# Two passes over 128 expert blocks: twelve blocks of activations kept on chip, and another pace for the work beside the first pass

## The chip, the cores and the metric

One core of one Trainium2 chip runs the whole program in one launch. The metric is the device time in microseconds; several runs of a kernel are compared by their median.

## The reference, cut to what matters

Two transformer blocks follow each other: one with a convolution, windowed attention and a layer of single-vector experts ("peer"), one with gated linear attention, sparse attention and feed-forward layers. The change lies in the expert layer:

```python
def peer(h, w_pq, sub_keys, u_emb, v_emb):
    q = (h @ w_pq).reshape(B, S, PEER_HEADS, 2, PEER_DHALF)
    sc = jnp.einsum("bshcd,hcnd->bshcn", q, sub_keys)
    s_top, i_top = lax.top_k(sc, PEER_TOPK)
    cand = s_top[..., 0, :, None] + s_top[..., 1, None, :]       # and its index
    best, pos = lax.top_k(cand, PEER_TOPK)
    gate = jax.nn.softmax(best, axis=-1)
    ...
    a = gelu(einsum("ced,cd->ce", u_emb[idx], hx))
    return einsum("ce,ced->cd", g * a, v_emb[idx])
```

There are 512 tokens of width 1024, 8 heads that choose 16 of 128 x 128 = 16384 experts each, and two tables, `u_emb` and `v_emb`, of 16384 rows of 1024 float32.

## The kernel before, in words

**Two ways to compute the layer.** For 352 tokens (`ND`) the kernel computes it densely: all 16384 activations, times a table of gates that is zero where an expert was not chosen. For the other 160 tokens it gathers the chosen rows: 128 tokens (`NF`) with one gather per chosen expert, 32 tokens (`NX`) packed four experts to a gather. That makes 128 + 32 = 160 gathers of rows of `u` and as many of `v`, each 128 rows of 1024.

**The dense passes.** Pass one runs over 128 blocks of 128 experts: `block` loads the block's weights of `peer_u` (SP's queue, three buffers `wr`), splits them into a high part `wh` (ACT, L195) and a low part `wl` (DVE, L196), and multiplies with the split tokens `hH`, `hL` in 24 matmuls of 128x352 (`three`, L216). ACT applies the gelu (L984) and stores the result to DRAM (`gd`, L985, ACT's queue). Pass two runs over the same blocks in the same order: it loads the activations of two blocks back (`g`), multiplies them with the table of gates (`w`, product `gw`, DVE, L1033), splits the product into `aH` and `aL`, and accumulates 24 matmuls with `peer_v` into eight PSUM tiles that stay open over all 128 blocks.

**Beside pass one.** A queue of small steps with costs, `self.queue`, holds what is left of the key search, the routing of each 128 tokens (`route`, DVE), and the build of the table (`spread_weights`): per four tokens a one-hot on DVE (L892, L900), others on ACT (L896, L897), eight small matmuls (L905), a copy on ACT (L906); every 16 tokens a store to DRAM (`wd`, L908). Each block of pass one runs `self.budget_u` units of that queue. Once the last 128 tokens are routed (`ready`), `chosen` issues gathers (POOL, L966) at `self.every(i)` rows a block, four buffers deep; a DVE instruction forms each dot (L943). In pass two the second gathers' rows are added up on DVE (L949), paced over all its blocks.

**Order of the work.** A planner lists the program's instructions by priority: `high_priority(n)` moves an instruction n places ahead in it, `issue_after` puts it behind another one on its engine. Each engine then works through its own list in order. Weights are `self.offset` = 90 places ahead, the loads of `g` and `w` `self.early` = 160, products and splits `self.soon` = 90. An engine with nothing due takes later work whose inputs are there. The loads of the table's first group of 16 blocks stand behind pass one in the program and are issued once the table is stored.

Of the kernel before, what the change touches and what calls it, by code (L numbers as in the profile page):

```python
# [22 lines left out]
S = 512  # L23
# [86 lines left out]
class Build:  # L110
    def __init__(self, ctx, tc, a, out):
        self.ctx, self.tc, self.nc, self.a, self.out = ctx, tc, tc.nc, a, out
        self.V, self.A, self.T, self.G = tc.nc.vector, tc.nc.scalar, tc.nc.tensor, tc.nc.gpsimd
        self.queue, self.rate, self.left, self.units = [], 0, 0, []
        self.waiting, self.rstd, self.behind = None, None, []
        self.lanes, self.credit, self.budget = [], 0, 0.8
        self.offset = 90
        self.early, self.soon, self.first = 160, 90, 60
        self.pad = 3.0

        self.on_act = lambda t: (0, 1) if t == 2 else (0, 1, 2)
        self.every = lambda i: 0.8 if i < 40 else 1.4 if i < 92 else 1.75
        self.wcost = 1.0
        self.rate_q = 4.5
        self.o2 = 40
        self.budget_u = 2.2
        self.ahead = 150
        self.sb = ctx.enter_context(tc.tile_pool(name="base", bufs=1))
        self.pp = ctx.enter_context(tc.tile_pool(name="psum", bufs=8, space=PSUM))
        self.dr = ctx.enter_context(tc.tile_pool(name="dram", bufs=1, space=DRAM))  # L130
# [542 lines left out]
    def peer(self, hs):  # L673
# [306 lines left out]
        next(rest)  # L980
        for i in range(NKEY):
            p = self.block(a["peer_u"][i], KD, hs, ND)
            g = self.tmp()
            A.activation(g[:, :ND], p[:, :ND], AF.Gelu)  # L984
            nc.scalar.dma_start(gd[i // 2][:, i % 2, :], g[:, :ND])  # L985
            self.run(self.budget_u)
            if len(self.queue) <= ready:
                budget += self.every(i)
            while budget >= 1.0 and sent < NF + NC:
                rest.send(self.last)  # L990
                sent += 1
                budget -= 1.0
        self.run()
        self.finish()
        inner.close()

# [15 lines left out]
        rounded = -(-ND // 64) * 64  # L1012
        wide = lambda tag, bufs, dt=F32: self.t(tag, rounded, bufs, dt, pool=pool)[:, :ND]
        for i in range(NKEY):

            with self.tc.high_priority(self.early):
                if i % 2 == 0:
                    g = self.t("g", 2 * ND, 3, pool=pool).rearrange("p (b n) -> p b n", b=2)
                    self.load(g, gd[i // 2])
                if i % NW == 0:  # L1020
                    w = ws.pop(0)
                    if i + NW < NKEY:
                        ws.append(weight_tile())
                if i % 2 == 0 and i // NW * NW + NW < NKEY:
                    with self.tc.issue_after(self.last_load):
                        part_of_weights(ws[0], i // NW + 1, i % NW // 2)
            with ExitStack() as near:
                near.enter_context(self.tc.high_priority(self.soon))
                if i < 2:
                    near.enter_context(self.tc.issue_after(end_u))  # L1030
                if i % 2 == 0:
                    gw = self.t("gw", 2 * ND, 2, pool=pool).rearrange("p (b n) -> p b n", b=2)
                    V.tensor_tensor(gw.rearrange("p b (u k) -> p b u k", k=TG), g.rearrange("p b (u k) -> p b u k", k=TG),  # L1033
                                    w[:, :, i % NW:i % NW + 2, :].rearrange("p u b k -> p b u k"), op=OP.mult)
                aH, aL = wide("aH", 3, F32R), wide("aL", 3, F32R)
                last = self.split(aH, aL, gw[:, i % 2, :])
            parts = self.weights(a["peer_v"][i], KD)
            for m in range(KD):
                self.three(acc[m][:, :ND], parts[m], (aH, aL), i == 0, i == NKEY - 1)
            while sent < min(n_sends, n_u + (n_sends - n_u) * (i + 1) / (NKEY - 3)):  # L1040
# [623 lines left out]
```

## Time and profile before

| what | us |
| --- | --- |
| median of 3 runs (3052.92 to 3059.8) | 3054.82 |
| the profiled execution | 3058.59 |
| its span | 3056.7 |
| PE busy in the span | 2973.7 (97%) |
| DVE busy | 2211.8 (72%) |
| ACT busy | 1314.8 (43%) |
| POOL busy | 478.9 (16%) |

Times in the views below count from the span's start. A busy PE is not PE at its peak: matmuls overlap, so what PE loses in a stretch is read by counting its matmuls. PEclk is the share of its clock that was granted; DMA is the mean busy share of the 16 DMA engines.

### The profile page before, as it was taken

Reading aid. Unit: us, or ns where it says so; the run is one execution under the profiler, and the core shown is the slowest. Engines: PE = TensorE matmul, PEld = TensorE weight load, DVE = VectorE, ACT = ScalarE, POOL = GpSimd, SP = SyncE. Lnnn points to the kernel's source line nnn. Section 1 sums busy time; section 2 is a strip of 40 time slices with the busy share of each in tenths; the row PEclk is TensorE's granted clock in tenths of the full one; section 3 lists DMA queues with packets and bytes.
Section 4 is the critical chain, followed back from the end, with each engine's and each line's share of the span. In section 5 each row is a group of like instructions: output and inputs, shape, how many; then the busy total and the mean of one; then the engine's idle time right before and its main releaser. Section 6 shows DMA issues by size and latency. Waiting matters only on the chain.

```text
span 3056.7 us, 41903 instructions
## 1 busy us (share of the span) xinstructions
PE 2973.7 (97%) x15549; PEld 2598.2 (85%) x15549; DVE 2211.8 (72%) x4115; ACT 1314.8 (43%) x2310; POOL 478.9 (16%) x338
## 2 busy tenths in 40 slices
PE   8999999999999998999999999999999999999998
PEld 7877788898999988999999888887788877888887
DVE  6999868999878677899989744434976655544435
ACT  5347542347888433333333422224333354323223
POOL 0000000022433454555555000000000000000000
PEclk9999999999999999999999999999999999999999
DMA  5321232387999999999999322333223334222232
GB/s 179 104 77 62 69 97 89 107 273 245 357 350 349 378 372 381 390 398 400 399 398 382 104 97 98 102 114 99 77 76 104 131 104 131 96 97 97 92 96 103
DMA packets 201716, 586.28 MB, mean 192 GB/s; under 512 B 21016, under 2 KB 64344, under 8 KB 198696
## 3 DMA queue, kind: packets, MB, share of 16 engines
q1 hardware_dynamic: 128944, 361.47, 34.1%
q0 software_dynamic: 46480, 168.14, 14.8%
q10 hardware_dynamic: 26088, 54.01, 4.9%
q8 instruction: 122, 2.00, 0.3%
q14 instruction: 82, 0.67, 0.1%
HBM read 523.94 MB, written 60.29 MB: 191 GB/s over the span
## 4 chain that ended last, share of the span: by engine, by line
PE 62%; DVE 18%; DMA 8%; issue 7%; POOL 3%; ACT 2%; DVEq 0%; POOLq 0%; ACTq 0%; SPq 0%
PE ps L216 54%; DMA wr<-in_peer_v_dram 4%; DVE wl L196 4%; POOL row L966 3%; DVE c L488 3%; PE ps L905 2%; PE ps L1287 1%; DMA g<-gd 1%; DVE topi L720 1%; DVE row L943 1%; DMA row<-in_peer_v_dram,rows 1%; PE ps L1324 1%; DVE top L719 1%; DVE tok L949 1%; ACT wh L195 1%
## 5 line engine op out<-in xcount | busy, mean ns | idle before, releaser
L195 ACT CAST wh<-wr 128x1024 fp32r<-128x1024 f32 (+1 forms) x560 | 584.3, 1044 | 1410.5 <-PE ps L216 668.2
L216 PE MATMUL ps<-hH,wh 128*128 128x512 f32 (+1 forms) x2792 | 1039.8, 373 | 8.1 <-ACT wh L195 6.1
L216 PE MATMUL ps<-hH,wl 128*128 128x512 f32 (+1 forms) x2792 | 1026.0, 368 | 20.1 <-DVE wl L196 20.0
L216 PE MATMUL ps<-hL,wh 128*128 128x512 f32 (+1 forms) x2792 | 1022.5, 366 | 1.6 <-DVE hL L196 1.4
L196 DVE TENSOR_TENSOR wl<-wr,wh 128x1024 fp32r<-128x1024 f32 (+1 forms) x560 | 678.8, 1213 | 253.4 <-ACT wh L195 251.0
L216 PEld LDWEIGHTS ps<-hH,wl 128*128 128x128 f32 x2792 | 527.0, 189 | 97.5 <-DVE wl L196 27.7
L216 PEld LDWEIGHTS ps<-hH,wh 128*128 128x128 f32 x2792 | 527.3, 189 | 83.3 <-ACT wh L195 7.8
L216 PEld LDWEIGHTS ps<-hL,wh 128*128 128x128 f32 x2792 | 527.6, 189 | 72.1 <-DVE hL L196 3.5
L216 PE MATMUL ps<-aL,wh 128*128 128x352 f32 (+1 forms) x1376 | 469.1, 341 | 5.3 <-DVE aL L196 5.3
L216 PE MATMUL ps<-aH,wh 128*128 128x352 f32 (+1 forms) x1376 | 467.6, 340 | 3.3 <-ACT aH L195 2.0
L216 PE MATMUL ps<-aH,wl 128*128 128x352 f32 (+1 forms) x1376 | 468.4, 340 | 0.6 <-DVE wl L196 0.6
L966 POOL DMA_INDIRECT row<-in_peer_rows_dram,rows x128 | 172.8, 1350 | 933.1 <-DVE topi L720 615.7
L216 PEld LDWEIGHTS ps<-aL,wh 128*128 128x128 f32 x1376 | 258.6, 188 | 23.6 <-DVE aL L196 9.5
L216 PEld LDWEIGHTS ps<-aH,wh 128*128 128x128 f32 x1376 | 259.5, 189 | 18.0 <-ACT aH L195 2.6
L216 PEld LDWEIGHTS ps<-aH,wl 128*128 128x128 f32 x1376 | 258.5, 188 | 14.5 <-DVE wl L196 0.9
L966 POOL DMA_INDIRECT row<-in_peer_v_dram,rows x128 | 202.5, 1582 | 186.9 <-DVE tok L949 159.3
L943 DVE CUSTOM_DVE_ANT_0 row<-row,tok 128x1024 f32<-128x1024 f32 x160 | 193.2, 1219 | 43.2 <-DMA row<-in_peer_rows_dram,rows 25.0
L488 DVE SCALAR_TENSOR_TENSOR c<-up,cw,c 128x512 f32<-128x512 f32 x240 | 171.4, 743 | 0.8
L949 DVE SCALAR_TENSOR_TENSOR tok<-row,dots,tok 128x1024 f32<-128x1024 f32 x127 | 162.4, 1278 | 4.3 <-DMA row<-in_peer_v_dram,rows 3.6
L216 PE MATMUL ps<-c,wh 128*128 128x512 f32 x384 | 126.4, 410 | 0.0
L1099 DVE TENSOR_TENSOR tmp<-ps,rstd 128x512 f32<-128x512 f32 x44 | 30.4, 691 | 129.8 <-PE ps L216 129.8
L905 PE MATMUL ps<-ohr,ohl 128*128 128x128 f32 x704 | 96.2, 275 | 2.6 <-DVE ohl L900 2.0
(353 smaller groups left out, 3061.0 us busy)
## 6 DMA issues: line engine op xcount, KB each, us to landing
wr<-in_peer_u_dram SPq DMA_DIRECT2D x128, 512.0 KB, 5.8
wr<-in_peer_v_dram SPq DMA_DIRECT2D x128, 512.0 KB, 8.4
wr<-in_ffn_w_in_dram SPq DMA_DIRECT2D x88, 512.0 KB, 3.2
wr<-in_mix_w_in_dram SPq DMA_DIRECT2D x46, 512.0 KB, 3.3
gd<-tmp ACTq DMA_DIRECT2D x128, 176.0 KB, 5.7
wd<-wb ACTq DMA_DIRECT2D x22, 1024.0 KB, 6.8
g<-gd SPq DMA_DIRECT2D x64, 352.0 KB, 8.2
wr<-in_w_in_dram SPq DMA_DIRECT2D x42, 512.0 KB, 3.5
```

The source lines that it names most:

```text
L195: self.A.copy(H, src)
L196: return self.V.tensor_sub(L, src, H.bitcast(F32)).ins
L216: self.T.matmul(ps, l, r, start=first and i == 0, stop=last and i == 2)
L488: V.scalar_tensor_tensor(y, u[:, w:w + S], cw[:, i:i + 1], y, op0=OP.mult, op1=OP.add)
L719: V.max(v[:, o], sl)
L720: V.max_index(ix[:, o], v[:, o], sl)
L905: T.matmul(pw[:, k * 128:k * 128 + 128], l4[:, k], r4[:, k], start=True, stop=True)
L943: V.tensor_tensor_reduce(out=g, in0=g, in1=h, scale=1.0, scalar=0.0, op0=OP.mult, op1=OP.add, accum_out=d[:, j:j + 1])
L949: V.scalar_tensor_tensor(sums[-1], g, d[:, j:j + 1], sums[-1], op0=OP.mult, op1=OP.add)
L966: G.indirect_dma_start(out=g, out_offset=None, in_=tables[i], in_offset=at)
L1287: T.matmul(pv[t], l[:, tok[t]], rr[:, s], start=k0 + k + n == 0, stop=k0 + k == KD - 1 and n == 2)
L1324: T.matmul(p[:, t * 64:t * 64 + 64], E[:, tok[t]], ql[:, t * 64:t * 64 + 64], start=True, stop=True)
```

## The change

Three things change.

- Paces. Rows per block of pass one: 1.2 up to block 40 and 1.4 after, where they were 0.8, 1.4 (from 40) and 1.75 (from 92). Units of the queue per block: 2.6 until the last tokens are routed and 1.9 after, where they were 2.2.
- The last twelve blocks of pass one write their activations to six tiles in SBUF (`kept`) instead of DRAM. For that the queue is emptied and the routing's memory closed ahead of block 116, not behind block 127.
- Pass two takes the blocks in another order: 116 to 127 from `kept`, then 112 to 115, then 0 to 111. The six tiles then serve as buffers for the activations that are loaded (three before). The split halves `aH`, `aL` take the eight buffers `hH`, `hL`, which pass one's tokens held, in place of three of their own.

```diff
-        self.every = lambda i: 0.8 if i < 40 else 1.4 if i < 92 else 1.75
+        self.every = lambda i: 1.2 if i < 40 else 1.4
-        self.budget_u = 2.2
+        self.budget_u = 2.6, 1.9
@@ peer, pass one
+        NK, kept = 12, []
+        by_two = lambda tag, bufs, pool: self.t(tag, 2 * ND, bufs, pool=pool).rearrange("p (b n) -> p b n", b=2)
         for i in range(NKEY):
+            if i == NKEY - NK:
+                self.run()
+                self.finish()
+                inner.close()
+                near_far = stack.enter_context(self.tc.tile_pool(name="near", bufs=1, reuse_waits="tile", side="right"))
             p = self.block(a["peer_u"][i], KD, hs, ND)
-            g = self.tmp()
-            A.activation(g[:, :ND], p[:, :ND], AF.Gelu)
-            nc.scalar.dma_start(gd[i // 2][:, i % 2, :], g[:, :ND])
-            self.run(self.budget_u)
+            if i >= NKEY - NK:
+                if i % 2 == 0:
+                    kept.append(by_two("g", NK // 2, near_far))
+                g = kept[-1][:, i % 2, :]
+            else:
+                g = self.tmp()[:, :ND]
+            A.activation(g, p[:, :ND], AF.Gelu)
+            if i < NKEY - NK:
+                nc.scalar.dma_start(gd[i // 2][:, i % 2, :], g)
+            self.run(self.budget_u[len(self.queue) <= ready])
...
-        self.run()
-        self.finish()
-        inner.close()
@@ peer, pass two
+        order = [*range(NKEY - NK, NKEY), *range(NKEY - NW, NKEY - NK), *range(NKEY - NW)]
         ws = [weight_tile()]
         for q in range(4):
-            part_of_weights(ws[0], 0, q, 4)
+            part_of_weights(ws[0], NKEY // NW - 1, q, 4)
-        for i in range(NKEY):
+        for n, i in enumerate(order):
             with self.tc.high_priority(self.early):
-                if i % 2 == 0:
-                    g = self.t("g", 2 * ND, 3, pool=pool).rearrange("p (b n) -> p b n", b=2)
+                if n % 2 == 0 and n < NK:
+                    g = kept[n // 2]
+                elif n % 2 == 0:
+                    g = by_two("g", NK // 2, near_far)
                     self.load(g, gd[i // 2])
...
-                aH, aL = wide("aH", 3, F32R), wide("aL", 3, F32R)
-                last = self.split(aH, aL, gw[:, i % 2, :])
+                aH, aL = (self.t(tag, S, 8, F32R)[:, :ND] for tag in ("hH", "hL"))
+                last = self.split(aH, aL, gw[:, n % 2, :])
```

## Rows read from the trace of the kernel before

**Rows 1.** The page's part 4: chain that ended last, by line.
```profile
PE ps L216 54%; DMA wr<-in_peer_v_dram 4%; DVE wl L196 4%; POOL row L966 3%; DVE c L488 3%; PE ps L905 2%; PE ps L1287 1%; DMA g<-gd 1%; DVE topi L720 1%; DVE row L943 1%; DMA row<-in_peer_v_dram,rows 1%; PE ps L1324 1%; DVE top L719 1%; DVE tok L949 1%; ACT wh L195 1%
```
**Rows 2.** L216 by stretch: from:to, length, PE busy (count), PEld busy (count), PEclk, DMA, GB/s.
```profile
581.98:764.20 182.22, 161.31 (x960) 155.19 (x961) 0.99 0.71 239
764.20:1029.30 265.10, 222.04 (x1248) 198.45 (x1249) 1.00 0.96 352
1029.30:1195.69 166.39, 147.48 (x867) 140.92 (x866) 0.98 1.01 380
1195.69:1232.00 36.31, 31.87 (x193) 30.76 (x193) 1.00 1.02 381
1232.00:1704.20 472.20, 467.31 (x2882) 462.49 (x2880) 1.00 1.00 383
...
581.98:693.20 111.22, 109.23 (x673) 107.61 (x673) 1.00 0.70 233
```
**Rows 3.** The same columns for L905, the table's small matmuls.
```profile
581.98:764.20 182.22, 17.95 (x136) 17.14 (x136) 0.99 0.71 239
764.20:1029.30 265.10, 78.23 (x571) 74.80 (x569) 1.00 0.96 352
1029.30:1195.69 166.39, 0.00 (x0) 0.00 (x0) 0.98 1.01 380
...
581.98:693.20 111.22, 0.84 (x8) 1.00 (x8) 1.00 0.70 233
```
**Rows 4.** Chain that ended last from 900 us: start, length, what, count.
```profile
907.45 1.78 PE ps L905 x16
909.23 7.68 PE ps L216 x48
```
**Rows 5.** All engines: from:to, length, PE, PEld, DVE, ACT, POOL, PEclk, DMA, GB/s.
```profile
1029.30:1195.69 166.39, 147.48 (x867) 140.92 (x866) 115.67 (x164) 51.07 (x75) 84.00 (x62) 0.98 1.01 380
...
581.98:757.00 175.02, 166.86 (x1066) 164.42 (x1065) 174.26 (x527) 103.62 (x213) 35.30 (x25) 1.00 0.72 242
```
**Rows 6.** Waits of 1029.3 to 1195.69: who for whom, us, times, longest.
```profile
ACT wh L195 <- DMA wr<-in_peer_u_dram: 93.8, 30, 9.0
```
**Rows 7.** All engines, three short stretches: two clock drops, one without loads of the table.
```profile
758.00:761.40 3.40, 3.40 (x14) 3.40 (x13) 3.40 (x8) 1.34 (x5) 0.00 (x0) 0.50 0.82 249
1058.30:1065.20 6.90, 6.58 (x21) 6.13 (x22) 3.53 (x6) 1.43 (x3) 2.63 (x2) 0.51 1.05 392
...
1115.00:1166.70 51.70, 47.57 (x291) 46.26 (x290) 38.36 (x56) 17.24 (x25) 30.26 (x21) 1.00 1.00 378
```
**Rows 8.** DMA: a queue (packets, MB, share); issues (count, KB each, median us to landing).
```profile
q0 software_dynamic: 46480, 168.14, 14.8%
...
wr<-in_peer_u_dram SPq DMA_DIRECT2D x128, 512.0 KB, 5.8
...
gd<-tmp ACTq DMA_DIRECT2D x128, 176.0 KB, 5.7
...
w<-wd SPq DMA_DIRECT2D x2, 768.0 KB, 16.7
...
w<-wd SPq DMA_DIRECT2D x2, 640.0 KB, 14.9
```
**Rows 9.** Timeline of ACT from 1040 us: start, length, what, idle before and its releaser.
```profile
1057.22 1.04 ACT L195 CAST wh<-wr 128x1024 fp32r<-128x1024 f32 x1 [9.03 <-DMA wr<-in_peer_u_dram]
```
**Rows 10.** DVE by line, 585 to 760 us: busy us, mean ns, idle before.
```profile
L196 DVE TENSOR_TENSOR wl<-wr,wh 128x1024 fp32r<-128x1024 f32 x38 | 46.1, 1215 | 0.0
L943 DVE CUSTOM_DVE_ANT_0 row<-row,tok 128x1024 f32<-128x1024 f32 x21 | 25.5, 1217 | 0.0
```
**Rows 11.** The gathers' rows, landing: first 610 to 760, then 1035 to 1190 us.
```profile
DMA to landing us min/median/max: 4.8/6.0/8.8
...
DMA to landing us min/median/max: 6.1/8.1/10.2
```
**Rows 12.** Timeline at the hand-over from pass one to pass two, ACT.
```profile
1192.84 0.88 ACT L195 CAST aH<-gw 128x352 fp32r<-128x352 f32 x2 [9.30 <-DVE gw L1033]
```

More of the change, by code (lines that the diff above doesn't have):

```diff
@@ L1014, in peer @@
-        for i in range(NKEY):
+        for n, i in enumerate(order):
             with self.tc.high_priority(self.early):
-                if i % 2 == 0:
-                    g = self.t("g", 2 * ND, 3, pool=pool).rearrange("p (b n) -> p b n", b=2)
+                if n % 2 == 0 and n < NK:
+                    g = kept[n // 2]
+                elif n % 2 == 0:
+                    g = by_two("g", NK // 2, near_far)
                     self.load(g, gd[i // 2])
-                if i % NW == 0:
+                if n % NW == 0:
@@ L1021, in peer @@
                     w = ws.pop(0)
-                    if i + NW < NKEY:
+                    if n + NW < NKEY:
                         ws.append(weight_tile())
-                if i % 2 == 0 and i // NW * NW + NW < NKEY:
+                if n % 2 == 0 and n // NW * NW + NW < NKEY:
                     with self.tc.issue_after(self.last_load):
-                        part_of_weights(ws[0], i // NW + 1, i % NW // 2)
+                        part_of_weights(ws[0], n // NW, n % NW // 2)
             with ExitStack() as near:
@@ L1028, in peer @@
                 near.enter_context(self.tc.high_priority(self.soon))
-                if i < 2:
+                if n < 2:
                     near.enter_context(self.tc.issue_after(end_u))
-                if i % 2 == 0:
-                    gw = self.t("gw", 2 * ND, 2, pool=pool).rearrange("p (b n) -> p b n", b=2)
+                if n % 2 == 0:
+                    gw = by_two("gw", 2, pool)
                     V.tensor_tensor(gw.rearrange("p b (u k) -> p b u k", k=TG), g.rearrange("p b (u k) -> p b u k", k=TG),
@@ L1034, in peer @@
                                     w[:, :, i % NW:i % NW + 2, :].rearrange("p u b k -> p b u k"), op=OP.mult)
-                aH, aL = wide("aH", 3, F32R), wide("aL", 3, F32R)
-                last = self.split(aH, aL, gw[:, i % 2, :])
+                aH, aL = (self.t(tag, S, 8, F32R)[:, :ND] for tag in ("hH", "hL"))
+                last = self.split(aH, aL, gw[:, n % 2, :])
             parts = self.weights(a["peer_v"][i], KD)
             for m in range(KD):
-                self.three(acc[m][:, :ND], parts[m], (aH, aL), i == 0, i == NKEY - 1)
@@ L1040, in peer @@
-            while sent < min(n_sends, n_u + (n_sends - n_u) * (i + 1) / (NKEY - 3)):
+                self.three(acc[m][:, :ND], parts[m], (aH, aL), n == 0, n == NKEY - 1)
+            while sent < min(n_sends, n_u + (n_sends - n_u) * (n + 1) / (NKEY - 3)):
                 rest.send(last)
```

2 lines of the change are left out of this document (removed).

## The prediction

> **What bounds the kernel now.** I read the chain that ended last first: it is TensorE's (PE's) matmuls of the weight helper at L216 with 54% of the span, so the question is where PE is kept from them [rows 1]. I then cut the two passes of the experts into five stretches at whole blocks and asked for PE's work in each. A block of either pass is 24 matmuls of 128x352. Undisturbed, 48 of them take 7.68 us and 16 of the table's small matmuls 1.78 us [rows 4], so a block costs 3.84 us and a table matmul 0.111 us. The reader is to subtract, in each stretch, that price from its length [rows 2, 3]. The counts of L216 are exact multiples of 24 but for one to three matmuls that straddle a border.
> - Blocks 0 to 39 of pass one: 182.2 - 40 x 3.84 - 136 x 0.111 = 13.5 us lost.
> - Blocks 40 to 91: 265.1 - 52 x 3.84 - 571 x 0.111 = 2.0 us lost.
> - Blocks 92 to 127: 166.4 - 36 x 3.84 = 28.2 us lost.
> - The first 8 blocks of pass two: 36.3 - 30.7 = 5.6 us lost.
> - Its other 120: 472.2 - 460.8 = 11.4 us, or 0.095 us a block.
>
> Together 60.7 us, 2% of the span; no edit here removes a matmul, so this is all there is to win.
>
> The reasons differ. In the third stretch the 16 DMA engines are busy all the time at 380 GB/s while VectorE (DVE) is at 70% [rows 5]; ScalarE (ACT) waits 93.8 us there for weights that have not landed, up to 9.0 us at a time; the longest such wait ends at 1057 us [rows 6, 9], right after the first parts of the finished table are asked for, whose loads take 15 to 17 us to land [rows 8]. A stall there also drops the granted clock to 0.5 for 6.9 us, which costs about half of that, 3.4 us [rows 7]. In the first stretch it is DVE: 174.3 of 175.0 us busy up to 757 us [rows 5]; PE's losses come at its end, and a clock drop of 3.4 us with them [rows 7].
>
> **Pace of the rows.** A block of pass one moves one weight load (512 KB, 0.524 MB), one store of activations (0.180 MB) and some gathered rows; 168.14 MB for 320 gathers makes 0.525 MB each [rows 8]. Before, blocks from 92 on ask for 1.75 rows: 0.524 + 0.180 + 0.919 = 1.62 MB. At 378 GB/s, the rate of the quiet part of that stretch [rows 7], that takes 4.29 us against PE's 3.84. After, they ask for 1.4: 1.44 MB or 3.81 us, just inside. Up to block 40 the pace rises from 0.8 to 1.2, that is 0.4 x 32 = 13 rows, and one more or two because the last quarter's route is ready about two blocks sooner (2.6 units a block and not 2.2). So some 14 of the 160 rows move from the tail to the front; the total stays, and so does the pace of pass two.
>
> **The table's pace.** Adding the costs in the queue, with about 14 searches left over from before, gives some 195 units (the 14 is my choice: 195 / 2.2 = 89 blocks is where the table's matmuls end, none being left after block 92 [rows 3]). After: 9 x 2.6 + 90 x 1.9, so it ends near block 99. That is ahead of block 116, where the queue is now emptied by force, so that call finds nothing. The first group of table weights (4 parts, 2 x 768 + 2 x 640 KB = 2.88 MB [rows 8]) follows the table's end before, and I expect it to again, now near block 99.
>
> **The tail, blocks 92 to 127 after.** Up to 98 the table still runs: about 0.3 us lost. Blocks 98 to 115 at 3.81 us of transfers have no slack, so the burst of table weights comes on top: 2.88 MB / 378 = 7.6 us; small restarts as in pass two (0.095 a block) 1.7; one short clock drop, as the first of [rows 7], 0.5 to 1.7. In blocks 116 to 127 the stores are gone: 1.26 MB, 3.33 us, slack. Sum about 10.6 against 28.2: **-17.5 us**. Bounds: 4 if the burst finds cover, 16 if all of the stretch's clock drop returns and the burst costs what its neighbourhood did.
>
> **The front, blocks 0 to 39.** 14 more dots at 1.22 + 0.08 us are 18 us of DVE; the table's queue gives back about 6 units by then. A unit costs (174.3 - 46.1 for weights - 25.5 for dots) / 84 units, about 1.2 us, so 7 us [rows 5, 10]. DVE has no idle time in which to hide the net 11 us. But the routing of later tiles is pulled ahead there and is not due; it can simply run 11 us longer beside PE, so the saturated stretch grows from 175 to 186 us at its old rate of loss (13.5 / 182): 0.8 us. I take **+2 us**, nearer to that than to the full 18 us, because before, with DVE as full, PE lost only 111.2 - 672 x 0.160 - 8 x 0.111 = 2.8 us in the first 28 blocks, and the rest only where routing and table matmuls coincide [rows 2, 3]. Bounds -4 (table matmuls are thinner now) and +18. Queued behind a late dot on DVE is the weights' low part, for which PE waits. Blocks 40 to 98 keep 1.4 rows beside the thinner table: **+0.5**.
>
> **The hand-over.** Pass two begins with the twelve blocks whose activations were never stored: 12 x 0.180 MB written and read fall away, 4.3 MB, 11 us of DMA at 380 GB/s, over a stretch in which PE and not DMA is to set the pace. Before, ACT stood 9.3 us in front of the first product, which waited on loads [rows 12]; that wait goes, since the product's inputs are in SBUF. What is new: the split halves of pass two take the buffers of pass one's activations, so the first split waits for the last block's first three matmuls. It then has 3.84 - 0.48 us for its copy and subtraction (0.88 us for two copies, [rows 12]), and the next blocks' weight casts are behind it in ACT's queue; I cost that at 0 to +5 and take 0.5. The table part of the next group is loaded as before. Of the 5.6 us lost in the first 8 blocks I leave 1.6: **-4 us**, bounds -5 and +2.
>
> **The rest of pass two.** Eight buffers of splits where there were three, six pairs of activations where there were three; but a block's transfers are unchanged, and its 0.095 us of loss goes with weights that land late. **-0.5 us**, bounds -6 and +3. The reuse of the split buffers in the next layer costs nothing: its first needs the sum of all blocks anyway.
>
> **Sum.** -17.5 + 2 + 0.5 - 4 - 0.5 = -19.5 us. The profiled execution took 3058.59 us, 3056.7 of it span; the runs' median is 3054.82. The profiled one gives 3039.1, the median 3035.3; I give 3036 as the median after.
>
> **A rule against the change.** Gathers land in 6.0 us (median) in the stretch where DVE is always busy, and in 8.1 us where DVE has gaps and DMA is full [rows 11]: they follow DMA, not DVE. The Trainium skill, SBUF — State Buffer, section "SBUF: two separate sides", says that DMAs issued from GpSimd starve for descriptors while certain VectorE instructions hold a port that the two engines share. The trace here does not agree with it; what it would cost is rival 5.
>
> **The rivals.**
> 1. *Bytes rule throughout.* If DMA, and not PE, sets the pace in all of 764 to 1700 us (352 to 383 GB/s [rows 2]), evening out gains nothing and only the 4.3 MB count: -11 us, 3044. For it: ACT's waits for weights in pass two; against it: 2.0 us lost in blocks 40 to 91 at 352 GB/s. Chance 0.17.
> 2. *DVE becomes the bound in blocks 0 to 39 (slower).* All 18 us of moved dots lie on the path, with one more clock drop (1.7); the tail gains only 12 because the table's burst moves into it. Sum +8: 3063. It decides from the point where the front loses more than the tail and hand-over give, some 16 us. For it: DVE at 99.6%; against it: the routing that may slide. Chance 0.09.
> 3. *The turn costs a block.* Splits that wait for pass one's buffers hold weight casts behind them in ACT's queue: one block and a chain (3.84 + 2.2) and a clock drop, 8 us: 3044. Against it: 3.4 us of slack for 0.9 us of work. Chance 0.09.
> 4. *The forced end is real.* The table's work lags behind its plan and is still pending at block 116: the burst of weights meets the first pass's end, and 8 to 17 us of the gain go: about 3050. Against it: 99 is 17 blocks ahead. Chance 0.06.
>
> 5. *Gathers starve beside a full DVE.* Each of the 14 moved gathers lands late by one dot and holds DVE's queue for it, 14 x 1.3 = 18 us in place of the 2 at the front: 3036 + 16 = 3052. Against it: the 6.0 us. Chance 0.02.
>
> My forecast has 0.57: from 3026 to 3043.
>
> **How the numbers follow.** The measurement can tell about 0.2%, 6 us. Faster by more (under 3048.7): nearly all of the forecast, 0.54, most of rivals 1 and 3, 0.22, of 4 0.02: 0.78. Same: 0.13, from the edges of these and rivals 4 and 5. Slower: 0.09, rival 2. The range leaves out a tenth at each side: 3019 (front and pass two at their lower bounds) to 3055.
>
> **What the profile after would show.** Right: blocks 92 to 127 within 150 us and not 166; ACT's wait for weights of pass one there cut by more than half; the first loads of the table near block 99, with the one stall that is left beside them; no load of activations before the first product. Wrong: DVE full beyond 800 us with PE idle before its low weights (rival 2); 0.3 us a block still lost from 100 to 115 (rival 1); ACT idle before the first splits (rival 3); table matmuls after block 110 (rival 4).

## The result: 22 us slower, and where the time went

| | before | after |
| --- | --- | --- |
| median, us (6 runs each) | 3058.09 | 3080.26 |
| lowest to highest | 3052.92 to 3060.18 | 3076.19 to 3082.15 |
| the profiled execution | 3058.59 | 3076.19 |
| its span | 3056.7 | 3074.4 |
| first matmul of pass one to first of pass two | 613.7 | 597.9 |
| first matmul of pass two to its end | 508.5 | 540.5 |

The ratio after/before is 1.0073, 95% interval 1.0063 to 1.0083: slower, by more than the noise, where 3036 had been forecast. The profiled execution of the kernel after is the fastest of its six, so some 4 of the 22 us are in no trace. The two passes went opposite ways. Pass one gained 15.8 us, as the change meant it to; pass two lost 32.0 us; the difference, +16.2, is nearly all of the 17.6 us between the profiled executions.

First the matmuls of L216 in the kernel after, cut at the same blocks as [rows 2] (from:to, length, PE busy, PEld busy, PEclk, DMA, GB/s):

```profile
583.18:757.52 174.34, 159.67 (x960) 155.40 (x961) 0.98 0.80 283
757.52:1025.07 267.55, 224.11 (x1249) 201.32 (x1249) 0.99 0.92 342
1025.07:1181.09 156.02, 144.19 (x866) 139.66 (x866) 0.99 0.99 375
1181.09:1211.81 30.72, 30.72 (x194) 30.72 (x194) 1.00 1.03 402
1211.81:1721.59 509.78, 480.64 (x2881) 469.30 (x2880) 0.98 0.94 351
```

The table's small matmuls (L905) in the first three of them, the same columns, to set beside [rows 3]:

```profile
583.18:757.52 174.34, 13.72 (x108) 13.51 (x108) 0.98 0.80 283
757.52:1025.07 267.55, 69.10 (x489) 65.79 (x487) 0.99 0.92 342
1025.07:1181.09 156.02, 14.59 (x112) 13.96 (x111) 0.99 0.99 375
```

Priced as in the prediction (3.84 us a block, 0.111 us a table matmul; 108, 486 and 110 of the latter, straddlers left out), the stretches lose:

| blocks | lost before | lost after | change | predicted |
| --- | --- | --- | --- | --- |
| 0 to 39 of pass one | 13.5 | 174.3 - 153.6 - 12.0 = 8.7 | -4.8 | +2 |
| 40 to 91 | 2.4 | 267.6 - 199.7 - 53.9 = 13.9 | +11.5 | +0.5 |
| 92 to 127 | 28.1 | 156.0 - 138.2 - 12.2 = 5.6 | -22.5 | -17.5 |
| first 8 of pass two | 5.6 | 30.7 - 30.7 = 0.0 | -5.6 | -4 |
| its other 120 | 11.3 | 509.8 - 460.8 = 49.0 | **+37.7** | -0.5 |
| together | 61.0 | 77.2 | +16.2 | -19.5 |

(The losses before are those of the prediction but for a few table matmuls at a border; last digits are rounded.) One line decides the case: the 120 blocks on which the prediction spent two sentences. Who waits there, in the kernel after (who <- for whom: us in all, times, longest):

```profile
POOL row L966 <- DVE tok L949: 216.2, 118, 13.0
ACT hH L195 <- DVE gw L1045: 46.5, 14, 5.9
PEld ps L216 <- DVE wl L196: 38.0, 36, 4.5
DVE gw L1045 <- DMA w<-wd: 28.3, 6, 6.5
PE ps L216 <- DVE wl L196: 28.2, 26, 4.2
```

Before, PE waited for no low weights there; all that PE waited for in these blocks was 4.8 us, nearly all of it this line:

```profile
PE ps L216 <- DVE aL L196: 4.4, 9, 0.9
```

POOL's line is slack (it runs ahead of the rows' additions). The other four hang together. DVE waits 28.3 us in six places for a part of the table (`w<-wd`), in front of a product `gw`; PE waits for DVE's low weights `wl`. Nothing joins `wl` to the table but DVE's queue. DVE's timeline at one of the six places (start, length, instruction, idle before it and its releaser) shows how:

```profile
1359.77 1.22 DVE L196 TENSOR_TENSOR wl<-wr,wh 128x1024 fp32r<-128x1024 f32 x1
1366.20 1.69 DVE L1045 TENSOR_TENSOR gw<-g,w 128x704 f32<-128x704 f32 x2 [5.22 <-DMA w<-wd]
1367.82 1.22 DVE L196 TENSOR_TENSOR wl<-wr,wh 128x1024 fp32r<-128x1024 f32 x1
```

DVE stands idle for 5.22 us. The product it waits with is wanted by PE only some 20 us later, but the next `wl` is behind it in the same queue and is wanted at once. PE's timeline right after:

```profile
1369.09 0.43 PE L216 MATMUL ps<-hH,wl 128*128 128x352 f32 x1 [3.94 <-DVE wl L196]
```

And the chain that ended last in 1355 to 1375 us (start, length, what) runs through that load, not through weights:

```profile
1357.30 8.88 DMA w<-wd
1366.27 0.74 issue
1367.01 0.88 DVE gw L1045
1367.90 1.14 DVE wl L196
```

DVE waits like this at all seven borders between groups of 16 blocks, where the first product of a group needs the last of the eight parts of its table (at the sixth the view names no part; the six others are the 28.3 us). Three quantities tell how near that is; I worked them out from each product's, split's and load's start against the start of its block's first matmul (medians, us ahead of that block):

| kernel | splits `aL` | products | products at the seven borders | issue of a group's last part | wait of the seven, together |
| --- | --- | --- | --- | --- | --- |
| before | 1.6 | 11.7 | 11.7 | 24.6 | 0 |
| after | 20.7 | 30.8 | 19.6, after waiting | 28.5 | 32.8 |

Before, the group's last part lands 11.4 us (median) after its issue, 12.1 to 14.7 us ahead of its block, and the border's product starts 0.1 to 3.2 us after that landing: it fits, but only just. After, DVE comes to the product some 24 us ahead (19.6 plus its wait), and the part is not there yet.

The border wait is not all of the 37.7 us. It shows as lost time at the thirteenth block of a group, four ahead of the border: 22.9 us there in the kernel after and 1.5 before, summed over the groups. The other positions lose 25.9 us and 9.6 before. So some 21 of the 37.7 us lie where DVE is seen to wait, and some 16 elsewhere; what those 16 are was not traced.

### The profile page after: what moved, and what is told of

It reads as the page before. It is cut to its first block, busy times and chain, and to the rows that moved or that the text cites. A ratio compares the mean times of both kernels' runs of the same rounds, so it can differ in the third digit from the quotient of the medians.

```text
span 3074.4 us, 41728 instructions
## 1 busy us (share of the span) xinstructions
PE 2982.8 (97%) x15549; PEld 2607.0 (85%) x15549; DVE 2209.8 (72%) x4115; ACT 1317.1 (43%) x2310; POOL 483.5 (16%) x338
## 3 DMA queue, kind: packets, MB, share of 16 engines
q0 software_dynamic: 46480, 168.14, 14.7%
## 4 chain that ended last, share of the span: by engine, by line
PE 67%; DVE 17%; DMA 8%; issue 4%; ACT 3%; POOL 0%; SPq 0%; ACTq 0%; DVEq 0%; POOLq 0%
PE ps L216 59%; DVE wl L196 4%; DMA wr<-in_peer_v_dram 3%; DVE c L488 2%; DMA row<-in_peer_v_dram,rows 2%; PE ps L905 2%; PE ps L1299 1%; DMA w<-wd 1%; DVE tok L949 1%; DVE row L943 1%; DVE topi L720 1%; PE ps L1336 1%; DVE top L719 1%; DVE hL L196 1%; ACT wh L195 1%
## 5 line engine op out<-in xcount | busy, mean ns | idle before, releaser
L216 PE MATMUL ps<-hH,wl 128*128 128x352 f32 (+1 forms) x3816 | 1363.4, 357 | 36.7 <-DVE wl L196 36.6
L216 PE MATMUL ps<-hH,wh 128*128 128x352 f32 (+1 forms) x3816 | 1375.4, 361 | 4.9 <-ACT wh L195 2.8
L216 PE MATMUL ps<-hL,wh 128*128 128x352 f32 (+1 forms) x3816 | 1357.6, 356 | 1.5 <-DVE hL L196 1.4
L216 PEld LDWEIGHTS ps<-hH,wl 128*128 128x128 f32 x3816 | 723.6, 190 | 119.0 <-DVE wl L196 48.9
L216 PEld LDWEIGHTS ps<-hH,wh 128*128 128x128 f32 x3816 | 723.9, 190 | 81.8 <-issue 6.4
L216 PEld LDWEIGHTS ps<-hL,wh 128*128 128x128 f32 x3816 | 723.9, 190 | 71.9 <-DVE hL L196 3.2
L216 PE MATMUL ps<-aH,wh 128*128 128x512 f32 x352 | 136.9, 389 | 0.0
L216 PE MATMUL ps<-aL,wh 128*128 128x512 f32 x352 | 136.9, 389 | 0.0
L216 PE MATMUL ps<-aH,wl 128*128 128x512 f32 x352 | 136.9, 389 | 0.0
L216 PE MATMUL ps<-c,wh 128*128 128x512 f32 x384 | 126.3, 409 | 0.0
L905 PE MATMUL ps<-ohr,ohl 128*128 128x128 f32 x704 | 97.4, 275 | 2.0 <-DVE ohl L900 1.9
L905 PEld LDWEIGHTS ps<-ohr,ohl 128*128 128x128 f32 x704 | 93.3, 192 | 2.4 <-DVE ohl L900 2.4
L216 PEld LDWEIGHTS ps<-c,wh 128*128 128x128 f32 x384 | 72.1, 188 | 21.0 <-issue 5.5
```

Source lines behind the costliest of these rows:

```text
L216: self.T.matmul(ps, l, r, start=first and i == 0, stop=last and i == 2)
L905: T.matmul(pw[:, k * 128:k * 128 + 128], l4[:, k], r4[:, k], start=True, stop=True)
```

## The experiments

Theory A: the eight buffers of the split halves let splits and products run far ahead, so that the border's product stands in DVE's queue before its table part has landed. Theory B: it is the six tiles for `g` (three before) that let products run ahead. Theory C: the new order of the blocks, with the twelve kept ones in front. Beside these the front was in question: what the new paces cost there, and what they are worth alone. Each kernel was timed against the kernel before on its own chip; the medians of before are 3055.56 (e1 to e4), 3057.77 (e5 to e8) and 3055.24 (e9 and e10).

Lost time in the stretches of the kernels, priced as above (the first quarter of pass one is cut at block 28 here, since the losses sit there):

| kernel | median | ratio to before [95%] | 0 to 27 | 28 to 49 | 50 to 91 | 92 to 127 | first 8 | other 120 |
| --- | --- | --- | --- | --- | --- | --- | --- | --- |
| before | 3058.09 | | 2.8 | 11.0 | 2.1 | 28.1 | 5.6 | 11.3 |
| after | 3080.26 | 1.0073 [1.0063, 1.0083] | 8.8 | 7.8 | 6.1 | 5.6 | 0.0 | 49.0 |
| e1_ring3 | 3038.96 | 0.9948 [0.9928, 0.9968] | 8.8 | 7.8 | 6.2 | 7.2 | 0.2 | 8.3 |
| e2_g3 | 3083.17 | 1.0091 [1.0069, 1.0114] | 8.8 | 7.8 | 6.9 | 9.0 | 0.2 | 52.3 |
| e3_before_ring8 | 3095.02 | 1.0138 [1.0115, 1.0162] | 2.9 | 11.1 | 1.2 | 25.5 | 2.0 | 47.9 |
| e4_parts_early | 3062.85 | 1.0022 [1.0008, 1.0037] | 8.8 | 7.8 | 6.1 | 6.5 | 0.0 | 30.0 |
| e5_before_paces | 3043.63 | 0.9961 [0.9947, 0.9975] | 8.9 | 7.7 | 6.0 | 7.7 | 2.0 | 9.3 |
| e6_ring3_oldpace | 3056.32 | 0.9993 [0.9983, 1.0002] | 2.9 | 12.3 | 2.3 | 25.2 | 2.8 | 12.8 |
| e7_gw_behind | 3038.59 | 0.9944 [0.9928, 0.9961] | 9.0 | 7.8 | 6.2 | 6.7 | 0.2 | 9.6 |
| e8_ring3_front | 3038.79 | 0.9940 [0.9923, 0.9957] | 2.8 | 14.9 | 6.9 | 9.5 | 0.0 | 9.6 |
| e9_ring3_parts | 3034.69 | 0.9929 [0.9916, 0.9943] | 8.9 | 7.8 | 6.1 | 0.2 | 0.3 | 10.7 |
| e10_ring5 | 3076.18 | 1.0070 [1.0055, 1.0085] | 8.7 | 7.8 | 7.1 | 5.8 | 0.0 | 45.1 |

### e1_ring3: the kernel after, with three of the eight split buffers

```diff
+        ring = [[self.t(tag, S, 8, F32R)[:, :ND] for tag in ("hH", "hL")] for _ in range(3)]
-                aH, aL = (self.t(tag, S, 8, F32R)[:, :ND] for tag in ("hH", "hL"))
+                aH, aL = ring[n % 3]
```

> The changed kernel, but the split halves of pass two go round three tiles of hH and hL instead of eight; nothing else differs. Theory A (eight buffers let the planner put the first product of each group of 16 blocks some 20 us ahead of its block into DVE's queue, where DVE then stands until the group's last part of the table has landed, and PE's next low weights stand behind it): the waits of gw on w, 28 us in six of the seven borders after, go under 5 us, pass two takes 495 to 510 us and not 540, and the time is 3040 to 3050 (3058 before, 3080 after). Theory B (six tiles for loaded activations put their loads ahead of the table's parts on SP's queue): the waits stay, 3075 to 3085. Theory C (the new order of blocks and the loads that all begin once pass two runs): 3075 to 3085.

3038.96 us: 41 us less than the kernel after, by one number. Matmuls of L216 in blocks 92 to 127 and in the other 120 blocks of pass two (columns as above):

```profile
1027.67:1185.30 157.63, 144.53 (x865) 140.01 (x865) 0.99 0.99 372
...
1216.24:1685.36 469.12, 466.36 (x2881) 462.72 (x2880) 1.00 1.00 381
```

The 120 blocks take 469.1 us where they took 509.8, and the clock is whole. The waits of that stretch in e1_ring3:

```profile
ACT wh L195 <- DMA wr<-in_peer_v_dram: 230.5, 92, 4.9
...
DVE wl L196 <- ACT wh L195: 42.8, 40, 2.6
...
PEld ps L216 <- DVE hL L196: 5.9, 12, 0.9
```

No product waits for a table part. The splits run 1.6 us ahead of their blocks again, the products 11.8, the border's products 11.5; the last part is issued 24.5 us ahead, as before the change. All else of the change is still in this kernel, so B and C are worth nothing on their own; theory A predicted this (the time came out 1 us under its range). That the six tiles need the eight buffers to do harm is left for the next run.

### e2_g3: the kernel after, with three tiles for the loaded activations

```diff
-                    g = by_two("g", NK // 2, near_far)
+                    g = kept[n // 2 % 3]
```

> The changed kernel, but activations that are loaded in pass two go round three of the six kept tiles. Theory A (eight split buffers): pass two stays at 530 to 545 us, the time at 3070 to 3085. Theory B (the six tiles' loads delay the table's parts): the waits of gw on w vanish and the time falls to 3040 to 3050. In between if three tiles hold the products back as well, since a product needs its activations: then some 3055 to 3065.

3083.17 us, 1.0009 times the kernel after by medians: no gain. The waits in pass two are those of after, here put down in part to the weights' load that came last on the same queue (two of this view's lines):

```profile
DVE gw L1045 <- DMA wr<-in_peer_v_dram: 29.0, 5, 7.4
...
DVE gw L1045 <- DMA w<-wd: 7.0, 1, 7.0
```

The border's products are the same seven, 19.4 us ahead of their blocks after waiting 39.5 us together. Theory B is false.

### e3_before_ring8: the kernel before, with nothing but the eight split buffers

```diff
-                aH, aL = wide("aH", 3, F32R), wide("aL", 3, F32R)
+                aH, aL = (self.t(tag, S, 8, F32R)[:, :ND] for tag in ("hH", "hL"))
```

> The kernel before, but with the split halves of pass two in the eight buffers hH and hL in place of three of their own; paces, order and stores as before. Theory A: it alone makes pass two slower, by 20 to 35 us where activations run as far ahead, so 3075 to 3090; if the three tiles for activations hold the products to three pairs ahead, less, 3062 to 3075. Theory B and theory C: no change, 3055 to 3061.

3095.02 us: the old order, the old paces, three tiles for `g`, and 39 us slower than before. L216 in the other 120 blocks of pass two, and two of the waits there:

```profile
1227.08:1735.81 508.73, 480.49 (x2882) 468.68 (x2880) 0.98 0.96 357
```
```profile
ACT hH L195 <- DVE gw L1031: 41.9, 16, 5.4
...
DVE gw L1031 <- DMA w<-wd: 27.9, 7, 6.9
```

508.7 us, as in the kernel after (509.8), and the same wait in the same size (27.9 and 28.3). The splits run 20.8 us ahead, the products 30.5. The time lies 5 us above the range that theory A had given. With e1_ring3 this is the answer from both sides: the buffers alone take about 40 us, whatever else is in the kernel.

### e10_ring5: the kernel after, with five

```diff
-        ring = [[self.t(tag, S, 8, F32R)[:, :ND] for tag in ("hH", "hL")] for _ in range(3)]
+        ring = [[self.t(tag, S, 8, F32R)[:, :ND] for tag in ("hH", "hL")] for _ in range(5)]
```

> The changed kernel with the split halves round five tiles of hH and hL. Theory A, with a length: a product goes about as many blocks ahead as there are split buffers; the last part of a group lands some 4 to 5 blocks ahead of the group. Three buffers stay clear of it (3039), eight stand before it for 2 to 7 us (3080). Five come about even with it: waits of gw on w of 0 to 2 us a border, pass two 500 to 515 us, 3038 to 3055. If the cost grew with every buffer (bunching), it would be about two fifths of the way, 3055 to 3060.

The diff is against e1_ring3 (the ring is then taken as `n % 5`). I expected something between three and eight buffers; it was 3076.18 us, practically the price of eight. L216 in the 120 blocks:

```profile
1215.36:1721.21 505.85, 475.98 (x2882) 472.12 (x2880) 0.97 0.94 354
```
The waits of the products and of PE there (the last line from DVE's waits in a window that begins earlier):

```profile
DVE gw L1046 <- issue: 31.0, 5, 7.6
...
PE ps L216 <- DVE wl L196: 29.8, 8, 5.9
...
DVE gw L1046 <- DMA w<-wd: 14.8, 2, 7.7
```

Two of the seven waits are put down to the table part and five to no releaser at all. That they are the same shows in the landings: at all seven borders the group's last part lands 0.1 to 0.2 us before the product starts. One of the five, by the part's issue, its time to landing and the product on DVE:

```profile
1360.87 0.43 SPq L183 DMA_DIRECT2D w<-wd  x1
...
DMA to landing us min/median/max: 12.4/12.4/12.4
...
1373.36 0.89 DVE L1046 TENSOR_TENSOR gw<-g,w 128x704 f32<-128x704 f32 x1 [7.08 <-issue]
```

The miss made the mechanism plainer. The leads, worked out as above:

| kernel | split buffers | splits ahead | products ahead | border's products, after waiting | their wait, together |
| --- | --- | --- | --- | --- | --- |
| e1_ring3 | 3 | 1.6 | 11.8 | 11.5 | 0 |
| e10_ring5 | 5 | 10.4 | 20.3 | 18.8 | 45.8 |
| after | 8 | 20.7 | 30.8 | 19.6 | 32.8 |

Each split can start when the block that used its buffer is done, at most one block less than there are buffers ahead: 7.7, 15.4 and 26.9 us; the traces show 5 to 6 us less. A product has two buffers of two blocks each, so it can start when the split of three blocks earlier is done, that is some three blocks (11.5 us) ahead of the splits' lead, less a us or two: 11.8, 20.3, 30.8. In the two kernels with three buffers (before and e1_ring3) the last part lands 12.1 to 15.1 us ahead of its block and the border's product starts 0.1 to 3.2 us later, so 11.8 is just inside; 20.3 and 30.8 are not. The waits at the seven borders appear between three and five buffers (four was not tried). They do not grow from five to eight: 45.8 and 32.8 us. With five nearly all of the loss lies at the thirteenth block (41.3 of 45.1 us), with eight less than half (22.9 of 49.0); why the two come to nearly the same time is not shown.

### e7_gw_behind: eight buffers, but each product queued behind the low weights of the block before it

```diff
             with ExitStack() as near:
                 near.enter_context(self.tc.high_priority(self.soon))
                 ...
+                    near.enter_context(self.tc.issue_after(self.last))
                     gw = by_two("gw", 2, pool)
```

> The changed kernel with its eight split buffers, but each product of activations and table (and its split) stands on DVE behind the low weights of the block before its own, so it can't be put further ahead than those. Theory A (the place of the first product in DVE's queue is the cause, not the number of buffers): the waits of gw on w vanish, the lead of the products falls from some 31 to under 15 us, pass two takes 495 to 510 us, the time is 3036 to 3050. Rival (the shared buffers hH, hL themselves cost, by what else waits for them): 3065 to 3085.

3038.59 us: the eight buffers cost nothing if the products are kept back by hand (4.7 us ahead of their blocks, 4.4 at the borders, no wait for a table part). The splits come back with them, to 4.2 us ahead. L216 in the 120 blocks:

```profile
1213.97:1684.38 470.41, 468.23 (x2881) 462.61 (x2880) 1.00 1.00 380
```

It is a second, independent way to the 3039 of e1_ring3, and it takes the blame off the buffers themselves: their memory, their place and their wait for pass one are all still there. What costs is where the product, and its split with it, stand in the queue; it takes away both parts of the loss, at the thirteenth block and elsewhere.

### e4_parts_early: eight buffers, the table's parts asked for twice as early

```diff
-                if n % 2 == 0 and n // NW * NW + NW < NKEY:
+                if n % NW < NW // 2 and n // NW * NW + NW < NKEY:
-                        part_of_weights(ws[0], n // NW, n % NW // 2)
+                        part_of_weights(ws[0], n // NW, n % NW)
```

> The changed kernel with its eight split buffers, but the eight parts of a group's table are asked for in the first eight blocks of the group before it, one a block, and not one in two blocks over all sixteen. Theory A: the part that the first product waits for has landed some 25 us earlier, DVE no longer stands there, and pass two falls to 500 to 515 us, the time to 3040 to 3055; the eight blocks with one part each carry 0.18 MB more a block and may lose a few us of it again. Theory D (running far ahead itself is the cost, since dots, sums and products bunch up on DVE, whatever the table does): 3070 to 3085.

3062.85 us: 17 us better than after, 24 us worse than e1_ring3. The last part is now issued more than 50 us ahead of its border and no product waits for it. But the loss has only partly gone. All engines from the first to the eighth block of one group, and in the rest of it (length, PE, PEld, DVE, ACT, POOL, PEclk, DMA, GB/s):

```profile
1249.80:1280.50 30.70, 26.54 (x154) 24.06 (x152) 24.68 (x27) 10.10 (x14) 10.59 (x9) 1.00 1.04 397
1280.50:1316.40 35.90, 35.08 (x214) 34.40 (x215) 35.19 (x37) 12.92 (x18) 23.28 (x15) 1.00 1.01 387
```

In 30.7 us PE gets through 154 matmuls, 6.4 blocks, where 8 would fit, with DMA at 397 GB/s. In the rest of the group PE is full. By position in the group, summed over the groups, e4_parts_early loses 0.8 us at the thirteenth block, where the kernel after loses 22.9, and 25.6 in the second to eighth, where after loses 12.1 and before 5.0. So the border wait is curable from the load's side. What remains was in part there already: outside the thirteenth block after loses 25.9 us and e4_parts_early 29.1. The time lies between the ranges of theory A and of theory D (running far ahead is itself a cost); how much of the rest is the doubled rate of the parts and how much the run-ahead is not shown.

### e5_before_paces: the kernel before, with the new paces alone

```diff
-        self.every = lambda i: 0.8 if i < 40 else 1.4 if i < 92 else 1.75
+        self.every = lambda i: 1.2 if i < 40 else 1.4
-        self.budget_u = 2.2
+        self.budget_u = 2.6, 1.9
-            self.run(self.budget_u)
+            self.run(self.budget_u[len(self.queue) <= ready])
```

> The kernel before with the new paces of rows and table alone: order, stores, split buffers as before. If the tail of pass one was the rows' pace: blocks 92 to 127 lose 8 to 14 us in place of 28, blocks 0 to 91 some 3 to 7 more than their 16 (as in the changed kernel, 22.7), pass two stays at 505 to 510 us; 3040 to 3050 in all, against 3055 to 3058 before. If the tail was won by the twelve blocks that are not stored: blocks 92 to 127 still lose 20 or more, and the time is 3055 to 3063.

3043.63 us, 14 us faster than before. L216 in blocks 92 to 127, the first 8 and the other 120 of pass two:

```profile
1023.77:1181.89 158.12, 144.86 (x865) 140.05 (x865) 0.99 1.01 386
...
1181.89:1214.58 32.69, 31.37 (x195) 30.84 (x194) 1.00 1.02 388
1214.58:1684.65 470.07, 465.89 (x2881) 461.33 (x2880) 1.00 1.00 384
```

The tail loses 7.7 us in place of 28.1 with the activations still stored and loaded: the paces alone carry nearly all of what the change is worth. The first 8 blocks of pass two lose 2.0 here in place of 5.6, so the hand-over gains by the paces too.

### e6_ring3_oldpace: kept blocks and new order, three buffers, the old paces

```diff
-        self.every = lambda i: 1.2 if i < 40 else 1.4
+        self.every = lambda i: 0.8 if i < 40 else 1.4 if i < 92 else 1.75
-        self.budget_u = 2.6, 1.9
+        self.budget_u = 2.2, 2.2
```

> The changed kernel with three split buffers and the old paces: what is kept on chip, the new order and the early end of the routing stand alone. If the paces win the tail: blocks 92 to 127 lose 18 to 26 us, the first 8 blocks of pass two at most 1 where they lost 5.6, the rest of pass two some 8; 3043 to 3052. If the kept blocks win it: the tail loses under 12, 3035 to 3043. With the three split buffers and the new paces it was 3039.

The diff is against e1_ring3. 3056.32 us, ratio 0.9993 with 1 inside its interval: the kept blocks and the order, alone, give nothing that can be measured. L216 in blocks 92 to 127 and the first 8 of pass two:

```profile
1032.27:1195.69 163.42, 147.28 (x866) 142.28 (x865) 0.97 0.99 369
1195.69:1229.15 33.46, 31.25 (x193) 30.70 (x193) 1.00 1.03 393
```

I had expected 3043 to 3052. The hand-over does lose less (2.8 for 5.6, where at most 1 was expected), and the tail 3 us; the rest of pass two gives 1.5 of that back. Beside the new paces the kept blocks show a little more: e1_ring3 stands 4.7 us under e5_before_paces and their runs don't overlap (3037.8 to 3039.79 against 3041.73 to 3045.55), but on different chips, and the intervals of the two ratios do overlap. Theory C is false in any case: the order costs nothing.

### e8_ring3_front: three buffers, the old pace for the first 28 blocks

```diff
-        self.every = lambda i: 1.2 if i < 40 else 1.4
+        self.every = lambda i: 0.8 if i < 28 else 1.45
```

> The changed kernel with three split buffers and with 0.8 rows a block up to block 28 and 1.45 after (1.2 up to 40 and 1.4 after in the change). If the stall of 4.9 us near block 25 comes from DVE, filled by the moved rows' dots, so that the routing's transposes wait: blocks 0 to 27 lose 3 to 5 us and not 8.8; the tail a few us more than 7; 3034 to 3040 against 3039 with the change's paces. If it is chance in the planner's order: no change at the front, 3038 to 3046.

The diff is against e1_ring3. The front of after has one stall of note: PE's matmuls of the routing (`ps<-table,tk`, L874) stand in its queue ahead of the next block's, and wait for DVE, which is full of dots. PE's waits in 583 to 757 us of the kernel after (all lines over half a us):

```profile
PE ps L874 <- DVE tk L832: 4.9, 1, 4.9
```

With the old pace up to block 28 that stall is gone and the first 28 blocks lose 2.8 us again, but the next 22 lose 14.9 and not 7.8, among them one stall of 5.29 us at 797 us. L216 in blocks 0 to 39 and 40 to 91:

```profile
582.61:752.77 170.16, 159.30 (x961) 154.26 (x961) 1.00 0.80 271
752.77:1026.42 273.65, 226.60 (x1249) 204.49 (x1249) 0.98 0.93 342
```

3038.79 us, the same as e1_ring3 by medians: the stretch is shorter by 4 us in front and longer by 6 behind. (The profiled execution, 3044.44, is the slowest of the four, so a few us of these losses may be its own.) My reading, which no run isolates: the dots have to be done somewhere in a stretch where DVE has nothing to spare, and PE pays for about the same part of them.

### e9_ring3_parts: three buffers, the first group's table parts as eight loads beside the kept blocks

```diff
             if i == NKEY - NK:
                 ...
                 inner.close()
+                inner = ExitStack()
+                pool = inner.enter_context(self.tc.tile_pool(name="experts", bufs=1, reuse_waits="tile"))
+                NW, first_parts = 16, [0, 1, 2, 4, 5, 6, 8, 9]
...
+                ws = [weight_tile()]
...
+            if i >= NKEY - NK and i - NKEY + NK in first_parts:
+                with self.tc.issue_after(self.last_load):
+                    part_of_weights(ws[0], NKEY // NW - 1, first_parts.index(i - NKEY + NK))
...
-        for q in range(4):
-            part_of_weights(ws[0], NKEY // NW - 1, q, 4)
```

> The changed kernel with three split buffers, and the first group of the table loaded in eight parts beside blocks 116 to 125, whose activations aren't stored, in place of four parts as soon as the table is there. If the burst of 2.9 MB at full DMA is what blocks 104 to 115 lose (7 us in three kernels): they lose under 2, blocks 116 to 127 up to 4, the time is 3033 to 3038 (3039 with the burst). If those blocks lose it to the rows alone: 5 to 8 us stay there, some more come at 116 to 127, 3039 to 3045.

The diff is against e1_ring3. 3034.69 us, the best of all: its five runs (3032.77 to 3035.04) lie under all of e1_ring3's, if on another chip. L216 in blocks 92 to 127:

```profile
1027.45:1178.05 150.60, 141.50 (x865) 138.15 (x865) 1.00 1.01 384
```

The last 36 blocks of pass one now lose 0.2 us; 7.2 us in e1_ring3 were the burst of four large parts, asked for as soon as the table was stored. The prediction's price for that burst (7.6 us) was right, and most of it could be had back (4.3 us by medians, on different chips), since the last twelve blocks store nothing and have DMA to spare.

## Why the prediction was wrong, step by step

**The bound: right.** PE's matmuls of L216 are the chain's largest share after as before (59% and 54%, [rows 1]), and the account by stretches adds up to the difference of the profiled executions.

**The table's pace: right.** The last table matmul falls in block 99, as worked out, and the first part of the table is asked for in the same block (before: 89 and 94). The queue is empty long ahead of block 116, so rival 4 did not happen.

**The tail: right in mechanism, 5 us under.** Predicted -17.5 with 10.6 us left; 5.6 were left. Blocks 92 to 103 and 110 to 127 lose 0.2 us together: at 1.4 rows a block the transfers are inside PE's time, as 3.81 against 3.84 us said, and none of the 1.7 us of small restarts came. Blocks 104 to 109 lose 5.4, the burst (7.6 predicted). ACT's wait for weights is down to a third of [rows 6]:

```profile
ACT wh L195 <- DMA wr<-in_peer_u_dram: 32.3, 13, 7.1
```

Rival 1, the bytes rule, falls with it: the first 8 blocks of pass two run at PE's pace at 402 GB/s, and in e1_ring3 the other 120 lose 8.3 us at 381.

**The front and the middle: mis-sized and misplaced.** 13 dots moved ahead of block 40, as worked out (14). The sum of the two terms was +2.5 and came out as +6.7, inside the bounds, but not as told: up to block 40 there was a gain of 4.8, where 28 fewer table matmuls and their one-hots fall (no run shows that this is the cause), and blocks 40 to 91 lost 11.5 more, of which the prediction had 0.5. The step that was mis-sized is "blocks 40 to 98 keep 1.4 rows beside the thinner table": in blocks 40 to 49 the table is not thinner (100 table matmuls there before and after), and those ten blocks lose 7.8 us for 0.3. DVE stays full into them, 71.7 of the 72.5 us from block 40 to 830 us, and PE waits twice for low weights:

```profile
PE ps L216 <- DVE wl L196: 4.9, 2, 2.7
```

A stretch of 3.4 us at half clock follows the first of the two. So the saturated stretch did grow, as the prediction said, but past block 40 and at 7.5 us where it had 0.8. This is the sign that the prediction gave for rival 2 (DVE full beyond 800 us with PE idle before its low weights), beside the 4.9 us stall in the fence of e8_ring3_front; rival 2's price of 18 us was not reached. Blocks 50 to 91 lose the other 4.0 more; at one place near 1012 us PE waits 1.9 us for a one-hot of the table and then runs 3.4 us at half clock, together 3.6 us.

**The hand-over: right in size, only partly for the reason given.** Predicted -4 with 1.6 us left; 0.0 was left, with nothing of rival 3: ACT has its half of the first two splits done 2 us ahead of pass two's first matmul, with no idle time in front of it where [rows 12] had 9.30 us:

```profile
1178.24 0.87 ACT L195 CAST hH<-gw 128x352 fp32r<-128x352 f32 x2
```

The 5.6 us are a little beyond the bound of -5. The eight blocks run at 3.84 us each, with DMA at 402 GB/s. But the prediction gave the gain to the activations that are not stored and loaded, and e5_before_paces, where they all still are, loses only 2.0 us there: the paces alone carry 3.6 of the 5.6. That part was luck.

**The rest of pass two: wrong, and the whole of the miss.** The step that failed reads: "Eight buffers of splits where there were three, six pairs of activations where there were three; but a block's transfers are unchanged" and takes -0.5 us, bounds -6 and +3. It was +37.7, some 21 of it at the block where DVE stands in front of a border's product. The step priced the buffers by what they move, which is nothing, and did not ask what they let go ahead. No rival had this mechanism: rival 3 looked at the same buffers, but at the one moment when pass one gives them up. Of the rows needed, the order was visible: the products of before could be seen 12 us ahead of their blocks, the table's parts one per two blocks with the last issued 24.6 us ahead and landing 11 us later, so that 1 or 2 us were to spare. What was missing was the question of what is behind the product on DVE, namely the low weights that PE needs at once.

**The sum.** With the one term taken out, the prediction comes near: e1_ring3, which is the change with the old number of split buffers, stands at 3038.96 us against the forecast 3036, 16.6 us under the kernel before on its chip where 19.5 had been summed. That is no credit to the forecast as made, whose range ended at 3055. Nor were the other steps all priced right: by the stretches of e1_ring3 the front and middle are off by +4.4 us, the tail by -3.4, the hand-over by -1.4 and the rest by -2.5, and part of this cancels.

What stays open: why the kept blocks are worth 4.7 us beside the new paces and 1.4 beside the old (both near what can be told), whether four buffers would do, and what the 16 us are that the kernel after loses in pass two outside the thirteenth blocks.

## What to carry to other kernels

A buffer more is an order more: where a planner or a scheduler lists instructions by when their inputs and buffers are there, more buffers on one tile pull its producers ahead on an in-order engine, and an instruction that then waits there for a transfer holds up everything behind it. So for each buffer count that a change raises, follow the chain of producers back, note how far ahead of its use each now stands, and compare that lead with the landing time of whatever it needs; here the waits begin somewhere between 11.8 and 20.3 us ahead, with landings 12 to 15 us ahead where nothing waited, and they do not grow from there. Prices by stretch, with the undisturbed block as the unit, carried over well and also found the one place where work was left to gain (the burst that e9_ring3_parts spread).

## What the runs showed of the hardware

**A short stall is paid twice, the second time through the clock.** In the other 120 blocks of pass two PE has five idle gaps of over 1.5 us, 1.9 to 4.2 us long; after each of them its granted clock stands at 0.5 for 3.4 us. In the front it stands at 0.5 for 6.8 us from the middle of the 4.9 us stall on. All engines of the kernel after in two such stretches (length, PE, PEld, DVE, ACT, POOL, PEclk, DMA, GB/s):

```profile
684.00:690.80 6.80, 4.30 (x15) 4.30 (x16) 6.80 (x23) 2.02 (x4) 3.32 (x3) 0.50 0.91 299
...
1370.10:1373.50 3.40, 3.40 (x14) 3.40 (x13) 3.40 (x5) 0.57 (x2) 2.13 (x1) 0.50 0.75 255
```

At half the clock, 1.2 GHz for 2.4, PE gets through about half the work: in the second row, in which PE is busy throughout, 1.7 us are lost; in the first PE is busy for 4.3 us, so 2.2 are lost to the clock. Between 583 and 1720 us there are nine such stretches in the kernel after, which cost some 16 us together by that count, against two before (5 us). Five of them lie in the 120 blocks: 8.5 of the 49.0 us lost there are not waiting but running slowly afterwards.

**Gathers land hardly later beside a full DVE, but their issue can take longer.** In 610 to 760 us of the kernel after, with DVE busy for 148 of the 150 us and more dots and gathers than before, the gathers' rows land in 6.4 us (median); before it was 6.0 [rows 11], and in the quieter stretch (1025 to 1181 us) 8.2. The issuing instruction on POOL does feel DVE: in 610 to 760 us of the kernel before it takes 0.94 us at the least, and 2.88 us all three times that it starts inside a DVE instruction of 2.28 us (L824). One of the three:

```profile
645.26 2.28 DVE L824 TENSOR_TENSOR eq<-tk,table 128x2048 bf16<-128x2048 f32 x1
...
645.48 2.88 POOL L966 DMA_INDIRECT row<-in_peer_rows_dram,rows  x1 [7.78 <-DVE tk L814]
```

The Trainium skill, SBUF — State Buffer, section "SBUF: two separate sides", says that DMAs issued from GpSimd starve for descriptors while VectorE runs instructions of certain kinds. These traces do not tell which of DVE's instructions are of that kind, so the prediction's "does not agree" says more than they show; they show only that none of these landings is late enough to matter.
